# The matrices of each recurrence block, made ahead of the scan of the block in front of it

## The chip, the cores and the metric

The kernel runs on one core of a Trainium2 chip. The metric is the device time of one execution in microseconds (us). Five engines work side by side: TensorE (PE, matmuls; PEld is its weight load), VectorE (DVE), ScalarE (ACT), GpSimd (POOL, here mostly an issuer of DMAs) and SyncE (SP, an issuer of DMAs). Each runs its own instructions in the order in which the compiler put them, and waits on semaphores for the others.

## The reference, cut to what matters

One layer of a hybrid encoder on 512 positions with 2048 channels. Of its two branches the second matters here, a diagonal complex state-space model with 64 groups of 16 channels and 64 states:

```python
h = rmsnorm(x, norm_g)
v, bg, cg, za, u, zb, ga, gb = split(h @ w_in)
ya = bg * causal_depthwise_conv(cg * v, conv_w)
ya = (ya * silu(za)) @ w_out_a
lam_bar = exp(lam * dt);  b_bar = (lam_bar - 1) / lam * b      # per group and state, complex
state_t = lam_bar * state_{t-1} + b_bar @ u_t                  # the recurrence, per group
yb = gelu(Re(c @ state_t) + d_skip * u_t)
yb = yb * sigmoid(yb @ w_glu + b_glu)
yb = (yb * silu(zb)) @ w_out_b
m = sigmoid(ga) * ya + sigmoid(gb) * yb
out = rmsnorm(x + m @ w_o, final_g)
```

## The kernel before

**Matmuls and weights.** Every large product is made in split precision: a weight tile `w_raw` is cast by ACT to `w_hi` (line 689), DVE takes the rest as `w_lo` (line 706), and three matmuls per k-tile are added up. `gemm` (line 854) takes one weight tile of 128 x 1024, issues 24 matmuls (lines 859, 860, 861) and then calls `step`. A projected row block of 128 channels, a "gate", takes two such calls, here called half-gates. `WStream` keeps the weights coming: at each `get` the load of the tile five places ahead is issued on SP (line 667), the cast three ahead and the rest two ahead; `w_hi` and `w_lo` have four buffers each.

**The recurrence.** The positions are cut into 128 chunks of T = 4. The 64 groups go in four blocks of 16 (class `Block`, 0 to 3). What one block does, in the units of its generators:

- `loads_u`, `loads`: 23 DMAs on POOL's queue for its parameters (`bc`, `bs`), its inputs (`ug`, `u4`) and shared coefficients (`wb`)
- `front`: on DVE, with ACT copies, the matrices `F` (output side), `bb` and `sl` (input side)
- `pe1`: on PE, 32 matmuls with `sl` (line 387, the chunk inputs) and 32 with `bb` and `F` (line 395, the kernel inside a chunk), into five PSUM tiles
- `post`: on ACT, copies of these into `h` (two tiles), `mi` and `el`
- `table`: on DVE, the rotation table `rr`, `ri` by doubling, levels 4, 5 and 6; ACT makes the first part and the decay `g`
- `scan`: on DVE, eighteen operations on 128 x 1024 elements, two of them scans along the chunks (line 483); its last one writes the states that `pe2` reads
- `skip`: on ACT, `d_skip * u` into `y`
- `pe2`: on PE, matmuls with `mi` (line 507) and `el` (line 510), into two PSUM tiles
- `result`: on DVE, the sum into `y`, and eight DMAs on POOL that store it

**The order.** The blocks are not a stage of their own. They are a background job (`bg`) that runs between the half-gates of the gate projections `gb` (16 gates) and `zb` (8): `step(5.5)` behind each half-gate lets the job go on until it has spent its money. A DVE operation of n elements per partition costs 0.1 + 0.001 n (line 58), a unit between two yields at least 0.6 (line 849); ACT, POOL and PE work costs nothing of its own. A unit that yields 1 makes the next step idle. The job's first part is `ssm_params`, then `ssm_blocks`, then `gelu`. The program's order is then the base for the compiler's scheduler, which may put an instruction that it expects to be ready ahead of one that it doesn't.

Before the change, the order for block i is: `front`; `pe2` of block i-1; table levels 4 and 5; `result` of block i-1; `pe1`; level 6; `post`; the loads of block i+1; `scan`; `skip`.

**Buffers.** All these tiles come from one SBUF pool of 37 buffers (`r4`, tag "r4"), as do the normed input `hp` (16 tiles, kept), `ssm_keep` and `ssm_base` (kept to the last block), `w_raw` and, during `zb`, four tiles `zb`. PSUM has eight tiles.

Of the kernel before, what the change touches and what calls it, by code (L numbers as in the profile page):

```python
# [1 line left out]

# [1 line left out]

# [531 lines left out]

def ssm_blocks(blocks):

    blocks[0].loads()
    yield 1  # L540
    for i, k in enumerate(blocks):
        yield from k.front()
        if i:
            blocks[i - 1].pe2()
            yield
        yield from k.table((4, 5))
        if i:
            yield from blocks[i - 1].result()
        k.pe1()
        yield from k.table((6,))  # L550
        yield from k.post()
        if i + 1 < len(blocks):
            blocks[i + 1].loads_u()
            blocks[i + 1].loads()
        yield from k.scan()
        yield from k.skip()
    yield 1
    blocks[-1].pe2()
    yield 1
    yield from blocks[-1].result()  # L560
# [162 lines left out]
def hybrid_kernel(ctx: ExitStack, tc: tile.TileContext, xT, x, cvec, fg, wu, wu7, wabc,  # L723
# [259 lines left out]
    blks = [Block(c, b, uy, scratch, bs_d, be_d, ce_d, dsk, msk) for b in range(NB)]  # L983
    blks[0].loads_u()
    bg.append(ssm_blocks(blks))
    bg.append(gelu(0, 8))

# [562 lines left out]
```

## Time and profile before

| | us |
|---|---|
| three runs, median (lowest, highest) | 1661.87 (1661.63, 1663.71) |
| the profiled execution, device time | 1661.74 |
| its span, first to last instruction | 1659.9 |
| PE busy in the span | 1636.8 |
| DVE, ACT, POOL busy | 1301.0, 797.6, 238.3 |

Positions in the profile are microseconds from the start of the span. The gate projections with the recurrence between them run from about 96 to 410 us; the four `pe1` begin at 163, 212, 272 and 331 us. A row of the timeline gives the start, the length, the engine, the line, the operation, what it writes and reads, its shape and its count; in brackets stands how long the engine was idle before it, and what ended that. A row of a table of waits gives who waited for whom, the total, the number of waits and the longest one. A row of stretches gives the busy time of each engine with its instruction count, then the granted PE clock (PEclk), the share of time that the DMA engines were busy, and GB/s.

### The profile page before, as it was taken

The numbers are of one execution on the slowest core, as the hardware profiler recorded it, in microseconds if no ns is written. First come the engines' busy times: TensorE is split into PE (matmuls) and PEld (weight loads), VectorE is DVE, ScalarE is ACT, GpSimd is POOL, SyncE is SP. The second block draws the span as 40 slices with busy tenths as digits, with TensorE's granted clock in tenths as the row PEclk, the third lists the DMA queues.
The fourth block names the chain that finished last, engine by engine and source line by source line (L and its number), as shares of the span: only waits on it lengthen the run. The fifth ranks groups of instructions, "written<-read, shape, count | busy, mean of one in ns | idle before, by whom it ended". The sixth has DMA issues, their size and how long they took to land.

```text
span 1659.9 us, 22983 instructions
## 1 busy us (share of the span) xinstructions
PE 1636.8 (99%) x8700; PEld 1397.8 (84%) x8700; DVE 1301.0 (78%) x1751; ACT 797.6 (48%) x1097; POOL 238.3 (14%) x387
## 2 busy tenths in 40 slices
PE   9999998899999999999999999999999999999997
PEld 7887887788888888888888888888888888888886
DVE  8996887895865687877878777777878787888497
ACT  6433556355522355555445555544545544446334
POOL 0012343211021101010100101001010231122000
PEclk9999999999999999999999999999999999999999
DMA  8333563543364677777776777777776788997783
GB/s 312 117 102 87 146 177 115 133 140 77 134 215 134 165 186 205 186 205 206 206 203 178 207 192 201 201 202 215 184 210 180 290 272 239 268 320 252 234 329 102
DMA packets 93199, 320.62 MB, mean 193 GB/s; under 512 B 12672, under 2 KB 12928, under 8 KB 93088
## 3 DMA queue, kind: packets, MB, share of 16 engines
q1 hardware_dynamic: 58752, 204.65, 35.8%
q0 software_dynamic: 33616, 113.40, 29.7%
q8 instruction: 68, 1.11, 0.3%
q10 hardware_dynamic: 720, 1.10, 0.2%
q14 instruction: 43, 0.35, 0.1%
HBM read 287.51 MB, written 25.30 MB: 188 GB/s over the span
## 4 chain that ended last, share of the span: by engine, by line
PE 94%; ACT 2%; DVE 2%; issue 1%; DMA 0%; DVEq 0%; SPq 0%; ACTq 0%
PE ps L1101 34%; PE ps L1106 18%; PE ps L1324 10%; PE ps L859 9%; PE ps L860 9%; PE ps L861 9%; PE ps L944 2%; PE ps L942 2%; PE ps L943 2%; PE ps L387 1%; PE ps L395 1%; ACT w_hi L689 1%; DVE ssm_t L66 0%; DVE w_lo L706 0%; PE ps L510 0%
## 5 line engine op out<-in xcount | busy, mean ns | idle before, releaser
L689 ACT CAST w_hi<-w_raw 128x1024 fp32r<-128x1024 f32 (+2 forms) x459 | 478.7, 1045 | 662.0 <-PE ps L1101 281.1
L706 DVE TENSOR_TENSOR w_lo<-w_raw,w_hi 128x1024 fp32r<-128x1024 f32 (+2 forms) x459 | 556.5, 1214 | 193.1 <-ACT w_hi L689 189.6
L1101 PE MATMUL ps<-h_comb,w_hi 128*128 128x512 f32 x1408 | 352.5, 392 | 0.0
L1101 PEld LDWEIGHTS ps<-h_comb,w_hi 128*128 128x128 f32 x1408 | 253.2, 189 | 45.2
L861 PE MATMUL ps<-pair,w_lo 128*128 128x512 f32 x720 | 280.7, 390 | 3.3 <-DVE w_lo L706 3.3
L859 PE MATMUL ps<-pair,w_hi 128*128 128x512 f32 x720 | 280.8, 391 | 3.2 <-ACT w_hi L689 2.7
L860 PE MATMUL ps<-pair,w_hi 128*128 128x512 f32 x720 | 280.4, 390 | 0.4 <-DVE pair L66 0.4
L1101 PE MATMUL ps<-pair,w_hi 128*128 128x512 f32 x1056 | 264.4, 392 | 0.0
L1101 PEld LDWEIGHTS ps<-pair,w_hi 128*128 128x128 f32 x1056 | 190.1, 189 | 34.1
L1106 PEld LDWEIGHTS ps<-h_comb,w_lo 128*128 128x128 f32 x1408 | 192.1, 190 | 13.7
L1106 PE MATMUL ps<-h_comb,w_lo 128*128 128x256 f32 x1408 | 196.3, 282 | 0.0
L859 PEld LDWEIGHTS ps<-pair,w_hi 128*128 128x128 f32 x720 | 135.0, 188 | 33.3 <-ACT w_hi L689 3.3
L861 PEld LDWEIGHTS ps<-pair,w_lo 128*128 128x128 f32 x720 | 135.1, 188 | 32.6 <-DVE w_lo L706 4.4
L860 PEld LDWEIGHTS ps<-pair,w_hi 128*128 128x128 f32 x720 | 135.2, 188 | 28.9 <-DVE pair L66 1.0
L1106 PEld LDWEIGHTS ps<-pair,w_lo 128*128 128x128 f32 x1056 | 144.1, 190 | 10.3
L1106 PE MATMUL ps<-pair,w_lo 128*128 128x256 f32 x1056 | 147.2, 282 | 0.0
L66 DVE TENSOR_TENSOR half<-ps,half 128x512 f32<-128x512 f32 x132 | 90.6, 686 | 66.5 <-PE ps L1106 66.5
L673 POOL DMA_DIRECT2D w_raw<-in_wabc_dram x64 | 55.2, 862 | 555.4 <-DMA w_raw<-in_wabc_dram 379.0
L1324 PE MATMUL ps<-w_hi,pair 128*128 128x512 f32 x192 | 60.8, 389 | 0.0
L597 DVE TENSOR_TENSOR w_raw<-w_raw 128x1024 f32<-128x1024 f32 x44 | 53.9, 1225 | 1.5
L593 DVE TENSOR_TENSOR w_raw<-w_raw 128x1024 f32<-128x1024 f32 x44 | 53.9, 1224 | 1.5
L1324 PE MATMUL ps<-w_hi,m_half 128*128 128x512 f32 x160 | 50.8, 389 | 0.0
(218 smaller groups left out, 1750.9 us busy)
## 6 DMA issues: line engine op xcount, KB each, us to landing
w_raw<-in_wabc_dram SPq DMA_DIRECT2D x160, 512.0 KB, 4.3
w_raw<-in_wga_dram SPq DMA_DIRECT2D x76, 512.0 KB, 5.1
w_raw<-in_wabc_dram POOLq DMA_DIRECT2D x64, 512.0 KB, 6.3
w_raw<-in_wo_dram SPq DMA_DIRECT2D x52, 512.0 KB, 6.1
w_raw<-in_wgb_dram SPq DMA_DIRECT2D x48, 512.0 KB, 3.8
w_raw<-in_wgz_dram SPq DMA_DIRECT2D x24, 512.0 KB, 3.4
w_raw<-in_wga_dram POOLq DMA_DIRECT2D x24, 512.0 KB, 7.1
m_r<-m POOLq DMA_DIRECT2D x32, 256.0 KB, 5.7
```

Of the source, the lines that this page charges most:

```text
L66: return v.tensor_tensor(out=o, in0=a, in1=b, op=op)
L593: tt(out=b11["x"], in0=b11["x"], in1=s1["x"], op=ADD)
L597: tt(out=s1["x"], in0=b12["x"], in1=b11["x"], op=ADD)
L673: nc.gpsimd.dma_start(box["x"], src.rearrange("p a b -> p (a b)"), accum_op=ADD)
L689: nc.scalar.copy(hi[:, a:b], raw[:, a:b])
L706: nc.vector.tensor_tensor(out=lo[:, a:b], in0=raw[:, a:b], in1=hi.bitcast(F32)[:, a:b], op=SUB)
L859: nc.tensor.matmul(ps, hi[:, k], a[:, 0], start=first and k == 0, stop=False)
L860: nc.tensor.matmul(ps, hi[:, k], a[:, 1], start=False, stop=False)
L861: nc.tensor.matmul(ps, lo[:, k], a[:, 0], start=False, stop=last and k == 7)
L1101: nc.tensor.matmul(ps if flat else both, hi[:, k], a, start=first and k == 0, stop=False, skip_group_check=True)
L1106: nc.tensor.matmul(ps[:, HL:], lo[:, k], a[:, :HL] if flat else a[:, 0], start=False, stop=last and k == 7, skip_group_check=True)
L1324: nc.tensor.matmul(ps, l, r[:, k2, c0:c1], start=first and k2 == i == 0, stop=last and k2 == 1 and i == 2, skip_group_check=True)
```

## The change

Only `ssm_blocks` changes. `front` of block 0 stands alone at the start. Then, for each block i:

- the loads of block i+1 are issued first, before the table of block i, where they stood behind its `post`
- table levels 4 and 5, then `pe2` of block i-1 (it stood behind `front` of block i), then level 6 (for the last block it stays behind `pe1`), `result` of block i-1 and `pe1` of block i
- `front` of block i+1, nine units, is interleaved with `post` of block i, six units: four of `front`, two of `post` (the copies into `h`), the rest of `front`, the rest of `post`
- `scan` and `skip` of block i

For the last block, level 6 takes the place of the next `front`. No operation is added or taken away, and no buffer count changes.

```diff
     blocks[0].loads()
     yield 1
+    yield from blocks[0].front()
     for i, k in enumerate(blocks):
-        yield from k.front()
+        last = i + 1 == len(blocks)
+        if not last:
+            blocks[i + 1].loads_u()
+            blocks[i + 1].loads()
+        yield from k.table((4, 5))
         if i:
             blocks[i - 1].pe2()
             yield
-        yield from k.table((4, 5))
+        if not last:
+            yield from k.table((6,))
         if i:
             yield from blocks[i - 1].result()
         k.pe1()
-        yield from k.table((6,))
-        yield from k.post()
-        if i + 1 < len(blocks):
-            blocks[i + 1].loads_u()
-            blocks[i + 1].loads()
+        f = k.table((6,)) if last else blocks[i + 1].front()
+        for _ in islice(f, 4):
+            yield
+        p = k.post()
+        for _ in islice(p, 2):
+            yield
+        yield from f
+        yield from p
         yield from k.scan()
         yield from k.skip()
     yield 1
```

More of the change, by code (lines that the diff above doesn't have):

```diff
@@ L1 @@
 from contextlib import ExitStack
+from itertools import islice
 import numpy as np
```

## The prediction

> **What bounds the kernel now.** Page first: span, busy times, slices, chain.
>
> ```profile
> span 1659.9 us, 22983 instructions
> PE 1636.8 (99%) x8700; PEld 1397.8 (84%) x8700; DVE 1301.0 (78%) x1751; ACT 797.6 (48%) x1097; POOL 238.3 (14%) x387
> ...
> PE   9999998899999999999999999999999999999997
> ...
> PE 94%; ACT 2%; DVE 2%; issue 1%; DMA 0%; DVEq 0%; SPq 0%; ACTq 0%
> ```
>
> PE is the bound: it is idle 23.1 us in all. The change adds and removes no matmul, so it can act only through PE's idle time and through matmuls that run slowly behind it. The two slices marked 8 (249 to 332 us) lie in the recurrence. The next view is who PE waits for, then PE in order of time at the rows that begin after a wait.
>
> ```profile
> PE ps L387 <- ACT ssm_sl L375: 6.3, 3, 3.0
> PE ps L861 <- DVE w_lo L706: 3.3, 3, 1.4
> PE ps L859 <- ACT w_hi L689: 2.7, 2, 1.6
> ```
>
> ```profile
> 163.22 3.49 PE L387 MATMUL ps<-ssm_ug,ssm_sl 64*128 64x128 f32 x32 [2.28 <-ACT ssm_sl L375]
> 166.65 2.76 PE L395 MATMUL ps<-ssm_f,ssm_bb 128*32 128x64 f32 x32
> ...
> 211.95 2.26 PE L387 MATMUL ps<-ssm_ug,ssm_sl 64*128 64x128 f32 x32
> 214.14 1.98 PE L395 MATMUL ps<-ssm_f,ssm_bb 128*32 128x64 f32 x32
> ...
> 256.06 0.50 PE L859 MATMUL ps<-pair,w_hi 128*128 128x512 f32 x1 [1.03 <-ACT w_hi L689]
> ...
> 261.35 0.50 PE L861 MATMUL ps<-pair,w_lo 128*128 128x512 f32 x1 [1.36 <-DVE w_lo L706]
> 268.38 0.50 PE L861 MATMUL ps<-pair,w_lo 128*128 128x512 f32 x1 [1.25 <-DVE w_lo L706]
> 271.55 2.69 PE L387 MATMUL ps<-ssm_ug,ssm_sl 64*128 64x128 f32 x32 [1.05 <-ACT ssm_sl L375]
> 274.17 1.97 PE L395 MATMUL ps<-ssm_f,ssm_bb 128*32 128x64 f32 x32
> ...
> 313.80 0.50 PE L859 MATMUL ps<-pair,w_hi 128*128 128x512 f32 x1 [1.62 <-ACT w_hi L689]
> 331.06 4.02 PE L387 MATMUL ps<-ssm_ug,ssm_sl 64*128 64x128 f32 x32 [2.99 <-ACT ssm_sl L375]
> 335.01 2.23 PE L395 MATMUL ps<-ssm_f,ssm_bb 128*32 128x64 f32 x32
> ```
>
> The pairs L387 and L395 are `pe1` of blocks 0 to 3. Three of four wait for `ssm_sl`, the last matrix that `front` makes; block 1 shows the undisturbed pair, 2.26 and 1.98 us. After a wait the same matmuls are slow, because the granted clock drops. In these stretches of 2 us it is the third number from the end:
>
> ```profile
> 166.00:168.00 2.00, 2.00 (x18) 1.78 (x16) 2.00 (x4) 1.93 (x5) 2.00 (x4) 0.50 0.38 127
> ...
> 332.00:334.00 2.00, 2.00 (x23) 2.00 (x22) 2.00 (x7) 0.92 (x2) 0.00 (x0) 0.54 0.57 205
> ```
>
> It is 0.50 and 0.54. Against block 1 the slow pair costs block 0 1.23 + 0.78 = 2.01, block 2 0.43 - 0.01 = 0.42, block 3 1.76 + 0.25 = 2.01 us. Wait and slow pair together: block 0 4.29, block 2 1.47, block 3 5.00 us. The waits for weights (`w_hi`, `w_lo`) are 1.03 + 1.36 + 1.25 + 1.62 = 5.26 us. All of it is 16.0 us, the most that there is to win in the recurrence.
>
> The Trainium skill (TensorE: Matmul & The Clock Gate, Part 1) says that the clock halves after an idle window of about 3.4 us. By that rule waits of 2.28 and 2.99 us need not cost clock, and blocks 2 and 3 would be worth the waits alone, 1.05 + 2.99 = 4.0 us, a time of 1657.7, inside the forecast's own range; the clock rows above differ from the rule.
>
> **The change part by part.** The order of instructions comes from the planner, so I count in its money. A DVE operation of n elements costs 0.1 + 0.001 n, each yield at least 0.6, and one half-gate of 24 matmuls hands out 5.5. `front` costs 10.6 (four of 0.74 to 1.48, then 1.37, 1.74, 0.6, 1.84, 0.6), `table` 3.64 for levels 4 and 5 and 3.67 for 6, `post` 6 x 0.6, `scan` 9 x 2.25 = 20.2, `skip` 1.2, `pe2` 0.6, `result` 1.2. A block is 44.7, eight half-gates before and after; from block 3's table on the units fall on the same half-gates as before.
>
> *`front` moved one scan forward.* Before, between the end of `front` and `pe1` stand `pe2`, levels 4 and 5 and `result`: 5.5, one half-gate. After, for blocks 1 to 3, the rest of `post`, a scan, `skip`, a table, `pe2` and `result`: about 29, over five half-gates. A half-gate lasts (254.48 - 243.60)/2 = 5.44 us by two tanh rows:
>
> ```profile
> 243.60 0.60 ACT L997 ACTIVATE tmp<-ps 128x512 f32<-128x512 f32 x1 [9.56 <-PE ps L861]
> 254.48 0.60 ACT L997 ACTIVATE tmp<-ps 128x512 f32<-128x512 f32 x1 [10.28 <-PE ps L861]
> ```
>
> The worst wait was 2.99 us, the added lead some 25 us: the `ssm_sl` waits of blocks 2 and 3 go, -1.47 and -5.00. Block 1 had none: 0. Block 0 has no scan in front of it; its `front` keeps its place and `pe1` moves only behind level 6, to the end of the half-gate where PE ran it already (160.9 us, where the 2.28 us wait began). Bounds 0 and -4.29; I take 0, the chain before it being untouched.
>
> *`pe2`.* It moves the other way: from `scan`'s last unit to `pe2` stood `skip` and the next `front`, 11.8; now `skip` and levels 4 and 5, 4.8. Block 0's last scan operations, and block 3's with its `pe2`:
>
> ```profile
> 196.56 2.46 DVE L66 TENSOR_TENSOR ssm_h<-ssm_h,ssm_t 64x1024 f32<-64x1024 f32 x2
> ...
> 364.60 2.47 DVE L66 TENSOR_TENSOR ssm_h<-ssm_h,ssm_t 64x1024 f32<-64x1024 f32 x2
> ...
> 376.85 0.44 PE L507 MATMUL ps<-ssm_u,ssm_mi 128*64 128x128 f32 x4
> ```
>
> Block 0's scan ended at 199.0. Now `front` of block 1 stands ahead of it. Its cost on DVE, from the stretch that it took, and the wait that it may fill:
>
> ```profile
> 170.20 3.75 ACT L419 ACTIVATE ssm_mi<-ps,cvec_t 32x512 f32<-32x512 f32 x8
> ...
> 176.95 2.36 DVE L706 TENSOR_TENSOR w_lo<-w_raw,w_hi 128x1024 fp32r<-128x1024 f32 x2 [5.02 <-ACT w_hi L689]
> ...
> 199.06 0.83 DVE L66 TENSOR_TENSOR ssm_ft<-ssm_bc,ssm_keep 128x640 f32<-128x640 f32 x1
> ...
> 210.12 0.69 DVE L66 TENSOR_TENSOR ssm_t<-ssm_t 128x512 f32<-128x512 f32 x1
> ```
>
> ```profile
> L689 ACT CAST w_hi<-w_raw 128x1024 fp32r<-128x1024 f32 (+2 forms) x459 | 478.7, 1045 | 662.0 <-PE ps L1101 281.1
> L706 DVE TENSOR_TENSOR w_lo<-w_raw,w_hi 128x1024 fp32r<-128x1024 f32 (+2 forms) x459 | 556.5, 1214 | 193.1 <-ACT w_hi L689 189.6
> ```
>
> 199.06 to 210.81, less two `w_lo` of 1.21 and a table operation of 0.2, is 9.1 us. With it, and two more `w_lo` (two half-gates later), the scan ends at 199.0 + 9.1 + 2.4 = 210.5. DVE's 5.0 us of idle time before 176.95 is a wait for a cast that ACT made behind `post`'s copies (the L419 row is the longest run of them); if `front` fills them, 205.5. PE reaches `pe2`'s place seven half-gates behind `pe1`: 169.4 + 7 x 5.44 = 207.5. Bounds of the wait: 0 and 3.0 us, plus clock. I take 0, because the compiler puts PE's matmuls where it expects them ready: by the planner block 0's `pe1` belongs at 155.5, and it stands one half-gate later, behind matmuls that were ready. What is late in its estimate costs nothing; only its error does.
>
> *Total DVE.* In 163 to 367 us:
>
> ```profile
> 163.00:367.00 204.00, 194.47 (x1149) 160.89 (x1150) 174.58 (x218) 106.21 (x192) 63.64 (x114) 0.98 0.53 142
> ```
>
> DVE is idle 29.4 us, PE 9.5. The last scan ends at 367.07 and its `pe2` comes at 376.85, so PE can gain 9.8 us before that scan is late even if DVE loses no idle time. Late next is this scan, then the gelu behind it.
>
> *Loads.* From the loads of the next block (23 POOL DMAs) to its `front` stood scan and `skip`, 21.4; now table, `pe2`, `result`, 9.1.
>
> ```profile
> 226.56 0.91 POOL L291 DMA_DIRECT2D ssm_bc<-in_ce_dram  x1
> ...
> 240.09 2.31 POOL L315 DMA_DIRECT2D ssm_u<-uy  x4
> ```
>
> ```profile
> DMA to landing us min/median/max: 2.7/4.1/8.1
> ```
>
> They take 15.8 us on POOL (226.56 to 242.40); the last row is the landing of `ssm_wb`, whose last DMA is issued by 240.09, 13.5 us in. `front` reads `ssm_bc`, the first load, at once, and `wb` only 6.9 later (four units, two of `post`, the 1.37): 16.0 of money against 13.5 and a landing of 4.1 to 8.1. Bounds: 0, and 5.7 us of DVE per block, which as DVE runs in order holds `w_lo` too. I take 0: POOL is busy 14% and starts as soon as buffers are free, ahead of the planner. Gate stores behind the loads have five `tmp` buffers, one used per 10.9 us: 0. PSUM: `pe1` holds five of eight banks for 11.8 rather than 4.9; gates need two: 0.
>
> *Buffers.* The pool has 37. `hp` (16), `ssm_keep` and `ssm_base` hold 18, the weight stream three `w_raw`. Before, at most 16 more are alive: the scan's 11 and five loads. After, at the table of block i+1: its rr, ri, t0, g, two F, bb, sl, ug, u4 (10), five loads, and u4, mi, el, h, x, y of block i (6): 21, so 39 with no `w_raw` at all. Allocations wait. Who waits already, on the SP queue from 163 to 340 us:
>
> ```profile
> SPq L667 <- DVE ssm_h L66: 27.7, 3, 13.2
> SPq L667 <- PE ps L510: 24.2, 3, 8.5
> ```
>
> Weight loads wait for recurrence tiles. The cover is their lead:
>
> ```profile
> 288.11 0.33 SPq L667 DMA_DIRECT2D w_raw<-in_wgz_dram  x1
> ...
> DMA to landing us min/median/max: 3.1/3.5/8.8
> ```
>
> The second row is the landing of all `w_raw` loads from 90 to 420 us. The load at 288.11 fed the matmul at 313.80, 25.7 us later. Needed at worst: landing 8.8, a tanh in front on ACT 10.28, cast 1.05, `w_lo` 1.21: 21.3. Bounds: the 5.26 us go because ready `pe1` matmuls fill them, or one half-gate is lost at each of three block borders, +16.3. I take 0.
>
> **Sum.** The profiled execution took 1661.74 us (span and 1.84), 0.13 under the median of the three runs. 1661.74 - 1.47 - 5.00 = 1655.3.
>
> **The rivals.** *More goes* (A): the weight waits too, 1650.0; block 0's as well, 1645.7. For it: `pe1` is ready long ahead. Against: more buffers are wanted. *The wait only moves* (B): `pe2` takes the place that `pe1` had, one half-gate behind a full DVE queue; three waits of 1.5, the middle of the bounds, with 1.2 of clock, the middle of 0.42 and 2.01, give +8.1, 1663.4. It decides when `front` doesn't fill DVE's idle time behind `post`. *Starved weights* (C), the other side: `w_raw` issues wait for the 21 tiles; -6.47 + 16.3 = +9.8, 1671.6. It decides once issues come more than 25.7 - 21.3 = 4.4 us later. For it the SP rows; against it that a `w_raw` granted right after `pe2` still has four half-gates, 22 us.
>
> The Trainium skill (Perfetto Trace Analysis, Optimization Strategy) says that the same gap coming back on the engine that should be full can mean that there is no SBUF for the next tile. By that rule the weight waits at 256 and 313 are shortage, and the change, which wants five tiles more, would go C's way; the SP rows agree as far as they go.
>
> **How the numbers follow.** Forecast 0.36, A 0.14, B 0.26, C 0.24. A measurement here can tell about 0.2%, 3.3 us. Faster: 0.36 + 0.14 = 0.50; within: most of B, 0.22; slower: C and the rest of B, 0.28. The range 1648 to 1669 leaves out A's far end and about half of C, some 0.17; the forecast's own is 1652 to 1658.
>
> **What would show it.** Right: no `ssm_sl` wait at the second to fourth L387 group, each pair near 4.2 us, the first still waiting about 2.3. B: waits of L510 or L507 for `ssm_h`. C: `w_hi` and `w_lo` waits of PE well over 5.3 us and `w_raw` issues less than 21 us ahead of use. If the last scan comes late, PE waits at the `pair` tiles of the gelu near 400 us.

## The result and the profile after

The changed kernel takes 1712.18 us (median of 4 runs, 1710.09 to 1713.07) against 1661.84 us before, measured beside it: a ratio of 1.0299 with an interval of 1.0281 to 1.0316. It is 50 us slower. 1655.3 was predicted, within 1648 to 1669. The profiled execution took 1711.97 us.

The page of the changed kernel; line numbers in it are one or eleven higher than before (L387 is now L388, L706 is L717):

```profile
span 1710.2 us, 22966 instructions
PE 1647.8 (96%) x8700; PEld 1405.0 (82%) x8700; DVE 1301.8 (76%) x1751; ACT 799.0 (47%) x1097; POOL 237.4 (14%) x387
```

The work of the engines is what it was (DVE 1301.8 and 1301.0 us busy). PE is idle 62.4 us and not 23.1, with the whole difference between 170 and 385 us, and it is busy 1647.8 us and not 1636.8 with the same 8700 matmuls. So of the 50.3 us that the span grew, 39.3 are idle time and 11.0 slower matmuls. Who PE waits for:

```profile
PE ps L872 <- DVE w_lo L717: 40.6, 7, 15.0
PE ps L870 <- ACT w_hi L700: 7.4, 3, 5.0
PE ps L388 <- ACT ssm_sl L376: 1.4, 1, 1.4
PE ps L508 <- issue: 1.3, 1, 1.3
```

Before, 6.3 us were for `ssm_sl` and 6.0 for the two halves of the weights; now it is 1.4 and 48.0. PE in order of time, at the rows behind a wait, and two `pe1` (the rows between them are left out):

```profile
163.16 2.69 PE L388 MATMUL ps<-ssm_ug,ssm_sl 64*128 64x128 f32 x32 [1.44 <-ACT ssm_sl L376]
190.94 0.79 PE L872 MATMUL ps<-pair,w_lo 128*128 128x512 f32 x1 [5.71 <-DVE w_lo L717]
211.47 0.50 PE L870 MATMUL ps<-pair,w_hi 128*128 128x512 f32 x1 [2.06 <-ACT w_hi L700]
212.72 2.06 PE L388 MATMUL ps<-ssm_ug,ssm_sl 64*128 64x128 f32 x32
214.70 1.97 PE L396 MATMUL ps<-ssm_f,ssm_bb 128*32 128x64 f32 x32
222.32 0.79 PE L872 MATMUL ps<-pair,w_lo 128*128 128x512 f32 x1 [5.64 <-DVE w_lo L717]
261.75 0.79 PE L872 MATMUL ps<-pair,w_lo 128*128 128x512 f32 x1 [5.57 <-DVE w_lo L717]
284.04 0.79 PE L870 MATMUL ps<-pair,w_hi 128*128 128x512 f32 x1 [5.00 <-ACT w_hi L700]
286.24 3.37 PE L388 MATMUL ps<-ssm_ug,ssm_sl 64*128 64x128 f32 x32
292.61 0.80 PE L872 MATMUL ps<-pair,w_lo 128*128 128x512 f32 x1 [2.44 <-DVE w_lo L717]
332.76 0.79 PE L872 MATMUL ps<-pair,w_lo 128*128 128x512 f32 x1 [5.57 <-DVE w_lo L717]
375.98 0.79 PE L872 MATMUL ps<-pair,w_lo 128*128 128x512 f32 x1 [15.01 <-DVE w_lo L717]
```

The second to fourth `pe1` wait for no `ssm_sl`, as forecast. In their place stand waits for `w_lo`, six in these rows and one of 0.7 us ahead of 150 us, and three for `w_hi`, two in these rows and one of 0.34 us. Three of 5.6 to 5.7 us come at about the same point of blocks 0, 1 and 2 (190.94, 261.75, 332.76), and one of 15.01 us at the end. The long idle stretches also lower the granted clock (third number from the end):

```profile
180.00:200.00 20.00, 14.29 (x52) 0.83 0.07 27
280.00:300.00 20.00, 13.53 (x78) 0.74 0.33 119
360.00:380.00 20.00, 4.75 (x23) 0.60 0.30 105
```

**Why `w_lo` comes late at 190.94.** The timeline of block 0 in the changed kernel, POOL, ACT and DVE:

```profile
152.33 0.92 POOL L292 DMA_DIRECT2D ssm_bc<-in_ce_dram  x1
...
165.15 1.15 POOL L316 DMA_DIRECT2D ssm_u<-uy  x2 [0.57 <-DMA ssm_wb<-ssm_scr]
...
178.92 0.60 ACT L1008 ACTIVATE tmp<-ps 128x512 f32<-128x512 f32 x1 [15.17 <-PE ps L872]
179.54 0.30 ACT L440 COPY ssm_rr<-ssm_base 128x128 f32<-128x128 f32 x1
...
179.88 0.29 DVE L67 TENSOR_TENSOR ssm_rr<-ssm_rr,ssm_keep 128x128 f32<-128x128 f32 x1 [16.28 <-ACT ssm_rr L440]
...
189.66 1.22 DVE L717 TENSOR_TENSOR w_lo<-w_raw,w_hi 128x1024 fp32r<-128x1024 f32 x1
```

and the same two operations before:

```profile
160.26 0.30 ACT L439 COPY ssm_rr<-ssm_base 128x128 f32<-128x128 f32 x1
...
160.88 0.28 DVE L66 TENSOR_TENSOR ssm_rr<-ssm_rr,ssm_keep 128x128 f32<-128x128 f32 x1
```

The copy that starts the table came at 160.26 and now comes at 179.54. It needs only constants. On ACT's queue it stands behind a tanh that waits 15.17 us for a gate to end on PE, and DVE, whose next instruction is the table, is idle for 16.28 us. Then the table, `front`, the scan and the weights all want DVE at once. DVE's busy time in two stretches of 20 us, after and then before:

```profile
160.00:180.00 20.00, 2.64 (x4) 1.00 0.61 138
180.00:200.00 20.00, 19.94 (x37) 0.83 0.07 27
```

```profile
160.00:180.00 20.00, 14.68 (x26) 0.91 0.55 135
180.00:200.00 20.00, 19.81 (x17) 1.00 0.55 146
```

DVE loses 12 us and `w_lo` at 189.66 is among what it does late.

**Why it stands there.** In the compiled order of both kernels, before and after, the first uses of the tiles of the pool `r4` follow the order in which the program asks for them; there are twelve exceptions, most of them tiles asked for together. (This is read from the compiled programs; a trace doesn't show it.) A tile has to wait its turn. The change asks for the five tiles of the loads ahead of the table's `rr`, `ri`, `t0` and `g`. POOL needs from 152.33 to 166.30, 14.0 us, to issue these 23 loads, so the table's tiles come after them, and the scheduler has by then put the tanh ahead of the copy. (This step is inferred from the order; `a_rr` below tests it.) Before, the first tile asked for behind the loads was the scan's `t1`, which needs no ACT copy.

**Why the others.** At the scans of blocks 0, 1 and 2 DVE waits for ACT's copies into `el`, 20.3 us in three waits (a row below): in the compiled program `t1` has the place of the block's first `F`, and that comes free only when `el` has read it. And SP, which fetches the weights through the same pool, waits more for DVE's operations on `t`, `t0` and `t1`, which the trace shows under one name:

```profile
SPq L678 <- DVE ssm_t L67: 105.9, 8, 34.3
SPq L678 <- DVE w_lo L717: 52.1, 5, 19.9
```

The first of these is 20.7 us before, the second 49.8. The wait of 15.01 us is the end of it: block 2's scan begins late, and `w_lo` of that half-gate stands behind it on DVE:

```profile
353.46 6.80 SPq L678 DMA_DIRECT2D w_raw<-in_wgz_dram  x3
...
358.50 1.23 DVE L67 TENSOR_TENSOR ssm_t<-ssm_h,ssm_ri 128x1024 f32<-128x1024 f32 x1 [6.36 <-ACT ssm_el L429]
...
374.70 1.23 DVE L717 TENSOR_TENSOR w_lo<-w_raw,w_hi 128x1024 fp32r<-128x1024 f32 x1
```

So there were two suspects, the *turn* (tiles handed out in order behind 14 us of loads) and the *places* (too few tiles in the pool), and a third, that it is merely the new order of `front`, `post` and scan on DVE and ACT. The experiments take them apart.

### The profile page after: what moved, and what is told of

Its sections match the earlier page's. It is cut to its first block, busy times and chain, and to the rows that moved or that the text cites. A ratio compares the mean times of both kernels' runs of the same rounds, so it can differ in the third digit from the quotient of the medians.

```text
span 1710.2 us, 22966 instructions
## 1 busy us (share of the span) xinstructions
PE 1647.8 (96%) x8700; PEld 1405.0 (82%) x8700; DVE 1301.8 (76%) x1751; ACT 799.0 (47%) x1097; POOL 237.4 (14%) x387
## 4 chain that ended last, share of the span: by engine, by line
PE 85%; DVE 5%; ACT 4%; issue 3%; POOL 1%; DMA 1%; SPq 0%; DVEq 0%; ACTq 0%; POOLq 0%
PE ps L1112 33%; PE ps L1117 17%; PE ps L1335 9%; PE ps L872 7%; PE ps L870 7%; PE ps L871 7%; PE ps L953 1%; PE ps L954 1%; PE ps L955 1%; DVE ssm_t L67 1%; DVE ssm_h L484 1%; DVE w_lo L717 1%; ACT ssm_mi L420 1%; DVE ssm_h L67 1%; ACT w_hi L700 0%
## 5 line engine op out<-in xcount | busy, mean ns | idle before, releaser
L717 DVE TENSOR_TENSOR w_lo<-w_raw,w_hi 128x1024 fp32r<-128x1024 f32 (+2 forms) x459 | 556.1, 1213 | 177.1 <-ACT w_hi L700 173.7
L872 PE MATMUL ps<-pair,w_lo 128*128 128x512 f32 x720 | 285.6, 398 | 40.6 <-DVE w_lo L717 40.6
L870 PE MATMUL ps<-pair,w_hi 128*128 128x512 f32 x720 | 285.0, 397 | 8.0 <-ACT w_hi L700 7.4
L871 PE MATMUL ps<-pair,w_hi 128*128 128x512 f32 x720 | 284.6, 395 | 0.4 <-DVE pair L67 0.4
L1112 PE MATMUL ps<-pair,w_hi 128*128 128x512 f32 x1056 | 264.4, 392 | 0.0
L1112 PEld LDWEIGHTS ps<-pair,w_hi 128*128 128x128 f32 x1056 | 190.0, 189 | 34.1
L872 PEld LDWEIGHTS ps<-pair,w_lo 128*128 128x128 f32 x720 | 138.0, 192 | 71.8 <-DVE w_lo L717 43.1
L870 PEld LDWEIGHTS ps<-pair,w_hi 128*128 128x128 f32 x720 | 138.0, 192 | 38.8 <-ACT w_hi L700 8.4
L871 PEld LDWEIGHTS ps<-pair,w_hi 128*128 128x128 f32 x720 | 137.8, 191 | 30.4 <-DVE pair L67 1.0
```

What stands on the lines that cost most here:

```text
L717: nc.vector.tensor_tensor(out=lo[:, a:b], in0=raw[:, a:b], in1=hi.bitcast(F32)[:, a:b], op=SUB)
L870: nc.tensor.matmul(ps, hi[:, k], a[:, 0], start=first and k == 0, stop=False)
L871: nc.tensor.matmul(ps, hi[:, k], a[:, 1], start=False, stop=False)
L872: nc.tensor.matmul(ps, lo[:, k], a[:, 0], start=False, stop=last and k == 7)
L1112: nc.tensor.matmul(ps if flat else both, hi[:, k], a, start=first and k == 0, stop=False, skip_group_check=True)
```

## The experiments

Ratios are to the kernel before, run beside each on the same chip, with their 95% intervals.

### More places

To free places without more memory, the last `hp` tiles of the norm are written into the ones in front of them, whose results are lost (the shift is 5 in `a_hp5` and in the control, 2 in `a_hp2`):

```diff
-            h = pair()
+            h = hp[k - 5] if k >= KD - 5 else pair()
             split(h, t)
```

**The changed kernel with five more places** (`a_hp5`).

> The changed kernel with five more buffers free in the pool r4: the last five of the sixteen `hp` tiles are written into the five tiles in front of them, so eleven tiles hold sixteen results (the output loses those five tiles; instructions and their order stay). Theory 1, the pool is short (21 tiles of the recurrence alive where 16 find a place, so that the allocation of w_raw, w_hi's partner and the h tiles holds whole queues): the waits for w_lo and w_hi at 190, 222, 261, 284, 332 and 376 us go, and the time falls from 1712 by some 45 to 57 us, to 1655 to 1667. Theory 2, the order on DVE and ACT (front's 9 us ahead of post and scan push w_lo back, whatever is free): the same waits stay, 1709 to 1715. A mixture of both stands between, 1680 to 1700.

1685.52 us, 1.0136 (1.012 to 1.0153): 26.7 us come back, about half. **With two more places** (`a_hp2`):

> The changed kernel with two more places instead of five (the last two `hp` tiles written over the two in front of them, which loses those two results). Five gave -26.7 us. If the loss from places grows with their number, two give about two fifths of it, 1697 to 1705; if the first places are worth the most, as in a queue that frees when one tile goes, 1686 to 1694; if a list of 42 needs all five, 1708 to 1713.

1682.23 us, 1.0121 (1.0106 to 1.0136). Two places give as much as five. **The control**, the kernel before with five more places (`b_hp5`):

> The control: the kernel before with the same five `hp` tiles written over the five in front of them. The pool was just enough before (37 of 37 at the peak), so both theories expect little: 1657 to 1663, the low end if some of the 5.26 us of waits for w_hi and w_lo came from the full pool. If the time falls by much more than 5 us, leaving tiles out changes more than the pool and the run beside it says less.

1653.29 us, 0.994 (0.9926 to 0.9953). The gain of before is real but small. Of the changed kernel's waits, DVE's wait for the table's copies stays, and so do PE's three waits at the same point of blocks 0, 1 and 2 (5.69, 5.56 and 5.57 us). The waits for `el` and PE's wait of 15.01 us have gone. The waits of DVE and PE in the kernel with five more places, 150 to 400 us:

```profile
DVE ssm_rr L67 <- ACT ssm_rr L440: 48.5, 3, 17.9
...
PE ps L872 <- DVE w_lo L717: 21.5, 7, 5.7
```

### The turn

**The table's tiles and their copies ahead of the loads** (`a_rr`), everything else as in the changed kernel:

```diff
         last = i + 1 == len(blocks)
+        yield from k.table((3,))      # takes rr, ri, t0, g and fills them, no level
         if not last:
             blocks[i + 1].loads_u()
```

> The changed kernel; the four tiles of the table (rr, ri, t0, g) are taken and filled by their copies ahead of the loads of the next block, and levels 4 and 5 stay behind the loads. Theory 3, the turn in the pool: tiles are handed out in the order of the program, so the table's tiles wait until POOL has issued the 23 loads in front of them (13.3 us at 0.53 to 0.91 us each); then the copies of rr fall behind a tanh that waits for the end of a gate, DVE stands still for 16.28 us, and w_lo comes 5.6 us late, once in each of blocks 0, 1 and 2 (190.94, 261.75 and 332.76 us, in the kernel with five more places at 191.79, 257.55 and 319.76). Without it those three waits go, with the slow stretch behind each: -17 to -25 us, 1687 to 1695. Theory 1, the full pool alone: four more tiles are held through the loads, so it is not faster, 1710 to 1725.

1686.17 us, 1.0146 (1.0129 to 1.0163): 26.0 us come back. The edit moves these copies past nothing but POOL's loads; among themselves the instructions of ACT, DVE and PE keep their order in the program. So it was the loads in front of them that made the copies late. The wait for `ssm_rr` is gone from DVE and so are the three waits of 5.6 us at PE; the wait for `el` and the long one at the end stay (line numbers are two higher again):

```profile
PE ps L874 <- DVE w_lo L719: 20.7, 3, 14.8
DVE ssm_t L67 <- ACT ssm_el L429: 20.2, 3, 7.0
```

**Both at once** (`a_rr_hp5`):

> The changed kernel with both remedies that gave something alone: the table's tiles taken and filled ahead of the loads (-26 us) and five more places (-27 us; the last five `hp` tiles written over the five in front of them, which loses those five results). If the turn behind the loads and the full pool are two causes that lie side by side, their gains add up: 1712.2 - 26.0 - 26.7 = 1659.5, so 1654 to 1665. If both remedies had only taken away the same waits, or if a third cause stays (front, post and the copies of h in one another's way, as 1689 for the loads behind `result` with the same places could mean), it stays at 1672 to 1688.

1661.92 us, 0.9993 (0.9982 to 1.0003). The two gains add up to within 2.4 us, and the changed kernel is level with the one before. The new order of `front`, `post` and scan costs nothing that would have to be explained by a third cause. PE's waits:

```profile
PE ps L874 <- DVE w_lo L719: 4.4, 3, 2.2
PE ps L872 <- ACT w_hi L702: 3.0, 2, 1.7
PE ps L388 <- ACT ssm_sl L376: 2.3, 1, 2.3
```

**The loads behind `result`** (`a_ldres`): they are moved behind the table, so the table has its turn first.

```diff
-        if not last:
-            blocks[i + 1].loads_u()
-            blocks[i + 1].loads()
         yield from k.table((4, 5))
...
             yield from blocks[i - 1].result()
+        if not last:
+            blocks[i + 1].loads_u()
+            blocks[i + 1].loads()
         k.pe1()
```

> The changed kernel with the loads of the next block behind `result` instead of in front of the table, so that the table has its turn in the pool ahead of them and the most tiles alive there fall from 21 to 16; at `front` and `post` 19 remain. Theory 3 (turn): the three waits of 5.6 us go, 1687 to 1695, and less where the shorter list also relieves the pool, down to 1665. Theory 1 (places): the four late w_lo and w_hi behind table and pe2 go, the ones behind front stay, 1680 to 1695. If front now comes too early for its own loads, PE waits for ssm_sl or for w_lo behind front, and it stays above 1700.

1711.7 us, 1.0297 (1.0281 to 1.0312): nothing gained. Of the three expectations only the number of the last came true. The timeline says why. Of the tiles behind the loads, the first that ACT fills are now `h` of `post`, and they take the place that `rr` had, behind a tanh:

```profile
191.36 0.60 ACT L1008 ACTIVATE tmp<-ps 128x512 f32<-128x512 f32 x1 [10.28 <-PE ps L872]
191.85 4.74 ACT L409 COPY ssm_h<-ps 64x512 f32<-64x512 f32 x8
194.24 1.23 DVE L67 TENSOR_TENSOR ssm_t<-ssm_h,ssm_ri 128x1024 f32<-128x1024 f32 x1 [13.27 <-ACT ssm_h L409]
```

The loads hold what comes behind them in line. **With five more places besides** (`a_ldres_hp5`):

> Both at once: the loads behind `result`, and five more places (the last five `hp` tiles written over the five in front of them, which loses those five of sixteen results). If turn and places are all that the change lost by, it comes down to the control of before with the same places, 1653.3, and below it by the waits for ssm_sl that the change takes away: 1648 to 1657. If it stays above 1665, there is a third cause in the order of front, post and scan itself.

1689.07 us, 1.0161 (1.0145 to 1.0177): the places are worth 22.6 us here too, the wait for `h` stays (39.8 us in three).

### The loads alone

**The kernel before with only the loads moved** (`b_ld`), from behind `post` to between `front` and `pe2`; `front` stays behind the scan.

```diff
         yield from k.front()
+        if i + 1 < len(blocks):
+            blocks[i + 1].loads_u()
+            blocks[i + 1].loads()
...
         yield from k.post()
-        if i + 1 < len(blocks):
-            blocks[i + 1].loads_u()
-            blocks[i + 1].loads()
         yield from k.scan()
```

> The kernel before with nothing but the loads of the next block moved, from behind `post` to the place behind `front` and ahead of `pe2` and the table; `front` stays behind the scan. Theory 3: the table's tiles wait for their turn behind 23 issues on POOL as in the changed kernel, in each of blocks 0 to 2, so the loss comes without front being moved: 1680 to 1710. Theory 2, front ahead of post and scan is what pushes w_lo back: 1660 to 1668.

1689.73 us, 1.0167 (1.0152 to 1.0182). The early loads bring half of the loss with no `front` moved. **With five more places** (`b_ld_hp5`):

> The kernel before with only the loads moved (1689.7), and five more places (the last five `hp` tiles written over the five in front of them, which loses those five results). It tells which of the two causes the early loads brought: if the table's turn behind 23 issues on POOL, the loss stays, 1675 to 1685 against 1653.3 for the same places without the move; if the full pool, it goes, 1652 to 1660.

1689.69 us, 1.0165 (1.0149 to 1.0182): no change, so this half isn't a matter of places. **With the table's tiles ahead of the loads** (`b_ld_rr`, the edit of `a_rr`):

> The other side of it: the kernel before with the loads moved, and the table's four tiles taken and filled ahead of them, no place added. Turn: the loss of 27 us goes, 1660 to 1668. Places: it stays or grows, since four tiles more are held through the loads, 1685 to 1700.

1682.26 us, 1.0118 (1.0101 to 1.0135): only 7.5 of 27 us come back, where 21 or more were expected. As in `a_ldres`, the copies of `h` are now the first behind the loads. DVE's long waits with the loads alone, then with the table's tiles ahead:

```profile
DVE ssm_rr L66 <- ACT ssm_rr L439: 53.6, 3, 18.9
```

```profile
DVE ssm_t L66 <- ACT ssm_h L408: 40.4, 3, 13.8
```

In `a_rr` the copies of `h` come late as well (182.82 us in block 0), but there DVE has `front` of the next block to do, and waits 0.7 us for them.

### What the kernels have in common

DVE's waits from 150 to 400 us (us; "-" where the list of waits has none):

| kernel | ratio | for copies of `rr` | for copies of `h` | for `el` (a place) |
|---|---|---|---|---|
| after | 1.0299 | 43.2 | 0.7 | 20.3 |
| `a_ldres` | 1.0297 | - | 39.9 | 20.2 |
| `a_rr_re1` (below) | 1.0189 | - | 7.0 | - |
| `b_ld` | 1.0167 | 53.6 | - | - |
| `b_ld_hp5` | 1.0165 | 53.1 | - | - |
| `a_ldres_hp5` | 1.0161 | - | 39.8 | - |
| `a_rr` | 1.0146 | - | 0.7 | 20.2 |
| `a_hp5` | 1.0136 | 48.5 | - | - |
| `a_hp2` | 1.0121 | 43.1 | - | - |
| `b_ld_rr` | 1.0118 | - | 40.4 | - |
| `a_rr_hp5` | 0.9993 | - | 1.2 | - |

A kernel with one of the two marks (a late ACT copy behind the loads, or the wait for `el`) is 1.2 to 1.7% slower, one with both 3.0%, and `a_rr_hp5`, with neither, is level. `a_rr_re1`, described below, doesn't fit: with little of either mark it is 1.9% slower, by other waits. Nor does the length of DVE's wait set the loss: 53.6 us go with 1.67%, 40.4 us with 1.18%, 20.2 us with 1.46%.

### Too few places in the order before

**Five tiles withheld** (`b_held5`).

> The kernel before, its order untouched, with five tiles of the pool r4 withheld from the start of the recurrence to its end (five tiles that GpSimd writes one column of at either end). Theory 1 (a shortage of five places is the cause by itself): the time rises by tens of us, 1690 to 1730, with waits of PE for w_lo and w_hi in the gates between 170 and 380 us. Theory 2 (order): 1660 to 1668, as SP only loads weights a little later.

1662.31 us, 0.9992 (0.9983 to 1.0002), but it says nothing: the tiles went back at once. The writes that were to hold them to the end of the recurrence were issued at 79.3 us, as the rows of the tile `held` show (the second is the closing write):

```profile
L988 POOL MEMSET held<- x5: 99/99/99, 67.7 to 73.8; 128x1 f32 x5
L558 POOL MEMSET held<- x5: 97/106/118, 79.3 to 79.5; 128x1 f32 x5
```

**Three tiles really withheld** (`b_hold3`), by a closing copy from the last block's `y`:

> The kernel before with three tiles of the pool withheld through the whole recurrence: ACT reads the `y` of block 3 into them at its end, so that they can't be given back early (a GpSimd write of a constant, tried first, gave them back at 79.5 us). Before needs 37 of 37 places where the loads of the next block are fetched. Places matter in any order: 1675 to 1700. Places matter only where `front` stands ahead of the scan and the loads ahead of the table, since the scan that waits in the order before has room behind it: 1660 to 1668.

1659.36 us, 0.9971 (0.996 to 0.9981). The closing copies come at 361.1 us, so the tiles were held. Three places fewer cost the order before nothing; it is even 0.3% faster, though five more also make it faster, by 0.6% (`b_hp5`). Places cost much only where `front` is made a scan ahead: there five of them bring back 22.6 to 26.7 us, with the loads behind the table too (`a_ldres`), and with the loads alone moved they bring back nothing.

### Versions that beat both

**Level 6 of the table ahead of `pe1`** (`b_t6`), in the kernel before:

```diff
-        k.pe1()
         yield from k.table((6,))
+        k.pe1()
         yield from k.post()
```

> The kernel before with one edit: level 6 of the table stands ahead of `pe1` and not behind it, and `front` stays where it was, so that no tile lives longer by more than one half-gate. If the waits for ssm_sl of blocks 0, 2 and 3 (2.28, 1.05 and 2.99 us, with the slow pairs behind them 10.8 us) come from too short a way from `front` to `pe1`, the added 5.4 us half-gate takes them away: 1651 to 1656. The rival: the copies of h now stand right behind `pe1` on ACT's queue and wait for it there, with w_hi behind them; then PE waits for w_hi in the half-gates after `pe1`, and the time is 1660 to 1668.

1655.59 us, 0.9958 (0.9945 to 0.9971). It gains 0.42%, 7.0 us, about what the change was priced at (6.47), with only part of the waits gone: block 2's goes, block 3's shrinks, block 0's stays (`ssm_sl` 4.1 us in all, 6.3 before). **With three tiles per block laid into tiles that are done** (`b_t6_re1`):

```diff
-        t1 = self.new([P, QB, NCH], "t1")
+        t1 = self.sl.rearrange("p q r s -> p q (r s)")
...
-        x = self.new([P, QB, NCH], "x")
+        x = rr
...
-        self.ysb = self.new([P, QB, NCH], "y")
+        self.ysb = ug
```

> The kernel before with level 6 ahead of `pe1`, and t1, x and y laid into sl, rr and ug as above, so that the pool is never full in the recurrence. With five places more the kernel before lost its two waits for w_lo (1.36 and 1.25 us) and most of its wait for ssm_sl in blocks 2 and 3; here the waits of 1.36 and 1.30 us for w_lo that level 6 left should go, with a slow stretch behind: 1649 to 1654. The rival: the copies into the reused tiles wait for readers (y for the loads of ug, x for the second turn), and the time is that of level 6 alone, 1655 to 1658, or worse.

1653.13 us, 0.9944 (0.9932 to 0.9957), the fastest kernel of the study. Only block 0's wait for `ssm_sl` is left; the waits for `w_lo`, which were expected to go, did not: they are 4.2 us in four:

```profile
PE ps L861 <- DVE w_lo L706: 4.2, 4, 1.4
PE ps L387 <- ACT ssm_sl L375: 2.3, 1, 2.3
PE ps L859 <- ACT w_hi L689: 1.6, 1, 1.6
```

**The same reuse in the changed kernel** (`a_rr_re1`, with the edit of `a_rr`):

> The changed kernel with the table's tiles ahead of the loads, and with three tiles of each block no longer taken from the pool but laid into tiles of the same block that are done: t1 into sl, x into rr, y into ug (in place). The result is complete. It frees about two places while the next block is loaded, and the scan and `skip` have no turn to wait for any more. Places as the cause of what is left: the wait of 14.79 us for w_lo in block 3, and those of 4.05 and 3.42 us, shrink: 1660 to 1675. If places weren't it: 1683 to 1688, as without the reuse.

1694.08 us, 1.0189 (1.0175 to 1.0203), 8 us slower than without the reuse: a miss. The wait for `el` as a place is gone, but PE now waits 37.9 us for `w_hi`, in three waits of 9.4 to 16.2 us, and SP's weight loads wait 45.7 us for DVE's last use of `sl`, which `t1` now keeps alive through the scan. (The wait of 14.79 us that was to shrink stood behind block 2's scan, not in block 3.) The reuse freed places at one point and held them at another; that this is all of the 8 us wasn't tested.

## Why the prediction was wrong

- *The `ssm_sl` waits of blocks 2 and 3, -6.47: right as to the waits.* None is left at the second to fourth `pe1`; block 1's pair takes 2.06 + 1.97 us, the first half of block 3's 2.06. Block 0 keeps one, 1.44 us and not 2.28. But block 2's pair is slow again (3.37 us for L388), now behind the wait of 5.00 us for `w_hi` at 284.04.
- *`pe2`, 0: right.* No wait of `pe2` for `ssm_h` shows, only 1.3 us of "issue". Rival B did not come.
- *Loads, 0: the first step that failed.* It asked only who reads the loads (`front`, 9.1 of money later), and covered the rest by "POOL is busy 14%". It did not ask who stands behind them in the line for tiles. The first behind them were the table's, with ACT copies that DVE waits for. Its upper bound of 5.7 us per block was near the 5.6 to 5.7 us of each of the three waits, but by chance: it was reckoned for late data of `front`. Measured: 26.0 us in the changed kernel, 27 with the loads alone moved.
- *Buffers, 0: the second step that failed.* The count of 21 tiles against 16 was right and so was the direction of its upper bound, +16.3. Measured: 22.6 to 30.0 us, over the bound, because the scans of three blocks themselves lost time (6 to 7 us each for `el`), not only one half-gate's weights. That two places gave as much as five shows that the count of 39 without any `w_raw` overstated the need.
- *Rival C* (starved weights, 1671.6, chance 0.24) named the right side, and its sign came: weight waits far over 5.3 us. It was mis-sized at +16.3 - 6.47: the two failed steps together are 49 to 57 us, and the whole change is +50.3. Its mechanism, weight loads held up by a full pool, is at most the half that more places bring back; the three waits of 5.6 us have another. The Trainium skill (Perfetto Trace Analysis, Optimization Strategy), cited there, says that a gap coming back can mean no room for the next tile. Here the gap that came back, those three waits, stayed with five more places and went with the turn. And of the weight waits that the prediction put down to shortage by that rule, those for `w_hi` at 256 and 313 us, 1.03 and 1.62 us, stand unchanged in the control with five more places (`b_hp5`).
- *The clock.* Stretches of 0.83, 0.74 and 0.60 granted clock are part of the 50 us, through the 11.0 us of slower matmuls; they follow the waits and were counted with them. The prediction counted 2.01 us each for the slow pairs of blocks 0 and 3. For block 0's that is the price in one execution and not of the wait: behind the same wait the clock falls in some traces and not in others (last section).
- *The end slack* (9.8 us before) is still there: the last scan ends at 417.39 us and its `pe2` begins at 427.05. The wait of 15.01 us stands behind block 2's scan, for whose delay the prediction had no term.

With both causes taken away (1661.92) the changed order is still no faster than before, and 8.6 us slower than the control with five more places (1653.29): waits of 9.7 us stand there against 6.3. The profiled executions, 9.9 us apart, show the rest: PE is idle 22.9 us against 17.7, and busy 4.7 us longer with the same matmuls, since the clock is halved three times between 190 and 340 us, for 3.4 us each, and not once there in the control.

## What to carry to other kernels

When a prefetch moves forward, don't stop at who reads it: list what stands behind it in every line that it joins, the issuing queue and the line for tiles of its pool, up to the first item on the critical path. A tile that only needs a copy of constants can be late by a whole gate if its turn comes behind 14 us of DMA issues. Before moving work a stage ahead, count the tiles alive at that point and try first what needs none: here a shift by one table level, and tiles reused inside their block, gave 0.56%, where the large move lost 3%.

## What the runs showed of the hardware that was not expected

Whether a short idle time costs PE its clock is not a matter of its length alone. Block 0's `pe1` waits 2.26 to 2.28 us for `ssm_sl` in twelve of the traces. In seven, the kernel before among them, the clock is halved behind the wait (0.50 from 166 to 168 us, and the pair takes 3.49 and 2.76 us); in five it is not. `b_t6` is one of the five:

```profile
163.12 2.69 PE L387 MATMUL ps<-ssm_ug,ssm_sl 64*128 64x128 f32 x32 [2.27 <-ACT ssm_sl L375]
...
166.00:168.00 2.00, 2.00 (x33) 1.87 (x31) 2.00 (x4) 1.94 (x4) 2.00 (x4) 1.00 0.35 115
```

Shorter waits can cost it too. The wait of 1.43 us in `a_hp5` does, and one of 1.44 us in the changed kernel does not:

```profile
162.43 3.87 PE L388 MATMUL ps<-ssm_ug,ssm_sl 64*128 64x128 f32 x32 [1.43 <-ACT ssm_sl L376]
...
164.00:166.00 2.00, 2.00 (x19) 1.99 (x17) 0.00 (x0) 0.00 (x0) 1.46 (x3) 0.50 1.08 244
```

Where the clock falls in the recurrence, it stays at half for 3.4 us or a whole multiple of that. The Trainium skill (TensorE: Matmul & The Clock Gate, Part 1) puts the idle window at about 3.4 us and calls it free-running. The traces agree with the length; that where a wait falls in the window decides would explain both outcomes, but no run here moves a wait within it. Waits of less than half of 3.4 us were enough here.

Of the compiler rather than the chip: a closing write of a constant does not keep a tile, since it is scheduled early: at 79.3 us in `b_held5`, where the end of the recurrence was meant.
